# A mixture-of-experts decoder layer on one core: output projection by row tile, held expert loads, an early first down-projection, three blocks combined at the end

## The chip, the core and the metric

The kernel runs on one core of one Trainium2 chip. The core has a matrix engine (TensorE, PE in the rows; its weight loads are PEld), a vector engine (VectorE, DVE), an activation engine (ScalarE, ACT), GpSimd (POOL) and a queue engine (SyncE, SP) that issues most of the transfers. Each engine executes its own instructions in the order written and waits only on semaphores. The metric is device microseconds (us) of one execution of the whole layer.

## The reference

One layer on 512 tokens of width 1024, all in f32: `x` is normalised, a mixer with three branches gives `m`, and two residual steps follow.

```python
x = layer_norm(ALPHA * x + m, ln1_g, ln1_b)      # m = y @ w_o + b_o, the output projection
f = hierarchical_moe(x, ...)                     # router: best of 4 groups, best 2 of its 4 experts
x = layer_norm(ALPHA * x + f, ln2_g, ln2_b)
```

There are 16 experts. Each has an up-projection (1024 to 2 x 256, SwiGLU) and a down-projection (256 to 1024), 3 MB of weights. Every token is worked on by two experts, with a weight for each.

## The kernel before, in words

All large products are done in three passes (`mm3`, L107): each f32 operand is split into a high part, rounded for TensorE (a cast on ScalarE), and a low part, the difference (a subtraction on VectorE). The products high-high, high-low and low-high are summed. So each expert weight that arrives by DMA costs one cast and one subtraction of 128x1024 per quarter of the up-projection (`prep_hi` L752, `prep_lo` L761) and the same for each half of the down-projection (`dn_hi` L1194, `dn_lo` L1199).

From the line `late.enter_context(tc.manual_schedule())` on, the order of every engine's instructions is the order in which the program writes them. A helper `weave` spreads independent instructions between those of a dependent chain. The stages of this part are:

1. **Output projection.** Eight steps `i` of the loop over `2 * NT`. Each is 24 multiplications of one row tile `t` (128 tokens) with one column half `n`. `wo_add` (L792) adds the residual from PSUM, `wo_stats` takes statistics, `r_tr` (L805) transposes the result on TensorE in the next step, and `router` (L813) multiplies it with the router weights. Before, `n` is the outer index: the four row tiles of the first half, then the four of the second. A row tile is complete only when its second half is done, so its layer norm (`ln1_stats`, `center_ops`, `scale_ops`), its stores (`put_x1`) and its routing (`route_ops`) lie in steps 5 to 7 and behind the loop.
2. **Routing.** `rank_mm` counts tokens per expert, `pos_ops` makes one-hot rows, and `pick` (L885) multiplies the normalised tokens with them, which gives the first block's tokens already transposed, without a trip through memory. The other blocks' tokens are fetched by `gather` (L1081, an indirect DMA on GpSimd from `x1_d`).
3. **Expert blocks.** 18 blocks of up to 128 tokens (`seq`; experts 15 and 14 have two blocks each). A block is `up_mm` (24 multiplications, L109), the gated activation `gate_h` (L1173, L1174), a transposition `h_tr` (L1180) and its split `h_ev`, and `down_mm` (12 multiplications, L1217). In block `b` the weights of the next expert are split, the tokens of `b + 1` are transposed and split (`transp`, L1159), and the down-projection of `b - 1` is done. `down_ev` copies the result and `scatter` (L1230) adds it into `acc_d` with an indirect DMA. Scatters follow one another: each waits for the one before to land, since both add into the same rows.
4. **End.** The last two blocks are not scattered. Their results are split (`down_split`) and added to the tokens by a product with one-hot rows (`row_hot`, `combine`), after the sum so far has been read back (`acc_load`). The second layer norm and the stores follow.

Loads of expert weights (`load_unit`, L747) go through SyncE's queue in program order. Each needs a free buffer of a pool (`o` five, `raw` two, `rawx` two, `raw3` one). The split parts lie in `xp` (four buffers) and `hlp` (five), both named `hl`.

Of the kernel before, what the change touches and what calls it, by code (L numbers as in the profile page):

```python
# [53 lines left out]
def trunk(ctx, tc, x, mem, rows, cols, wz, wkv, pac, pb8, pb2, wax, ws, wo, wr, br, we, out):  # L54
# [120 lines left out]
    acc_d = dram.tile([T, D], F32, name="acc_d")  # L175

# [524 lines left out]
    def load_xr(i):  # L701
        n, t = divmod(i, NT)
# [75 lines left out]
    for e, u in ((1, 0), (1, 1), (1, 2), (2, 0), (2, 2)):  # L778
        load_unit(e, u)
# [3 lines left out]
    def wo_mm(i, ps, k0, k1):  # L783
        n, t = divmod(i, NT)
# [5 lines left out]
    def wo_add(i, ps):  # L790
        n, t = divmod(i, NT)
        dve.tensor_tensor(x1[:, t, n * 512:(n + 1) * 512], ps, xrs[i], op=ALU.add)  # L792

    def wo_stats(i):
        n, t = divmod(i, NT)
# [4 lines left out]
    def r_tr(i):  # L800
        n, t = divmod(i, NT)
# [7 lines left out]
    def router(i):  # L809
        n, t = divmod(i, NT)  # L810
# [10 lines left out]
    def logits_b(t):  # L821
        dve.tensor_tensor(ge[:, t, :], ge[:, t, :], routed[NT + t][:, :20], op=ALU.add)
# [83 lines left out]
    rest = []  # L906
    pending = {NT: [(2, 1)], NT + 1: [(3, 0), (3, 1)], NT + 2: [(4, 0)]}
    for i in range(2 * NT):
        j = i - 1
        t = j - NT  # L910
        ps = mmps()
        if i == 6:
            ohe = so2.tile([P, NT, P], F32, name="xr2")
        wo_mm(i, ps, 0, 2)
        if i:
            r_tr(j)
        if i in (NT + 1, NT + 2):
            for h in range(2):
                prep_hi(0, 2 * (i - NT - 1) + h)
        wo_mm(i, ps, 2, 4)  # L920
        if i:
            router(j)
        if t == 0:
            weave(ln1_stats(0))
        elif t == 1:
            weave(ln1_stats(1), scale_ops(0, 256, range(0, D, 256)))
            put_x1(sp, 0)
        elif t == 2:
            ops, r_ = route_ops(0, 2)
            rest += r_  # L930
            weave(ops, ln1_stats(2))
        if t >= 0:
            logits_a(t)
            weave(center_ops(t, D, (0,)))
            logits_b(t)
            if t:
                weave(scale_ops(t, 512, (0, 512)))
                put_x1(sp, t)
        wo_mm(i, ps, 4, 6)
        if t == 2:  # L940
            rank_mm(0)
            rank_mm(1)
            ops, r_ = route_ops(2, 3)
            rest += r_
            weave(ops, pos_ops(0, 2)[:2])
        wo_mm(i, ps, 6, 8)
        for e, u in pending.get(i, ()):
            load_unit(e, u)
# [625 lines left out]
```

## Time and profile before

| | |
|---|---|
| time, three runs | 924.68 us median, 920.58 to 927.96 |
| profiled execution | 922.9 us, of which the span of the trace is 921.2 us |
| busy: TensorE, weight load | 879.5 us (95%), 730.1 us (79%) |
| busy: VectorE, ScalarE, GpSimd | 583.9 us (63%), 460.5 us (50%), 58.7 us (6%) |
| mean granted TensorE clock | 0.982 |
| moved by DMA | 145.10 MB, mean 158 GB/s |

The span runs from the first to the last instruction; the execution's own time is 1.7 us longer. TensorE is busy almost everywhere: in the page's 40 slices of 23 us only three, from 691 to 760 us, and the last two fall below 9 tenths. A share of busy time is an average: where TensorE idles, the rows below name what it waited for. In a timeline row the columns are start, duration, engine, line, operation, tiles, shape and count, and in brackets the idle time before it with the releaser.

### The profile page before, as it was taken

How to read it: one execution, taken by the hardware profiler on the slowest of the kernel's cores; microseconds unless marked ns; L12 is line 12 of the kernel's file. 1: busy time of each engine (PE TensorE's matmuls, PEld its weight loads, DVE VectorE, ACT ScalarE, POOL GpSimd, SP SyncE). 2: the span in 40 equal slices, each digit the busy share in tenths (PEclk: the TensorE clock that was granted, in tenths of full speed). 3: DMA queues.
4: the chain of work that ended last, by engine and by line, in shares of the span. 5: the costliest groups of instructions: out<-in, count | busy, mean ns of one | idle time of the engine just before them, and what ended most of it. 6: DMA issues, size and time to landing. Idle time of an engine off the chain costs nothing. (4 is left out here: it accounts for less than half of the span.)

```text
span 921.2 us, 11143 instructions
## 1 busy us (share of the span) xinstructions
PE 879.5 (95%) x4256; PEld 730.1 (79%) x4256; DVE 583.9 (63%) x1010; ACT 460.5 (50%) x656; POOL 58.7 (6%) x60
## 2 busy tenths in 40 slices
PE   9999999999999999999999999999997889999981
PEld 5778888889998888888788888788877678888860
DVE  6756773344555543345866765765288987689966
ACT  5545432223444432215678687533023657688943
POOL 0000100000000000000000000000000122323210
PEclk9999999999999999999999999999998999999995
DMA  8313633323222313321313331338572787889565
GB/s 340 121 46 115 228 115 108 116 97 125 104 92 97 137 46 98 115 80 64 123 58 103 137 104 58 99 131 336 238 281 94 265 324 281 280 277 408 143 178 139
DMA packets 29424, 145.10 MB, mean 158 GB/s; under 512 B 5507, under 2 KB 5763, under 8 KB 16309
## 3 DMA queue, kind: packets, MB, share of 16 engines
q1 hardware_dynamic: 21460, 127.25, 38.0%
q0 software_dynamic: 6192, 13.84, 5.9%
q10 hardware_dynamic: 1712, 3.24, 1.1%
q8 instruction: 35, 0.57, 0.3%
q14 instruction: 25, 0.20, 0.1%
HBM read 136.24 MB, written 17.83 MB: 167 GB/s over the span
## 5 line engine op out<-in xcount | busy, mean ns | idle before, releaser
L109 PE MATMUL mm<-hl 128*128 128x512 f32 x1416 | 327.6, 390 | 0.2 <-DVE hl L83 0.2
L109 PEld LDWEIGHTS mm<-hl 128*128 128x128 f32 x1416 | 264.6, 188 | 54.7 <-DVE hl L83 0.6
L83 DVE TENSOR_TENSOR hl<-raw,hl 128x1024 fp32r<-128x1024 f32 (+1 forms) x116 | 136.2, 1180 | 136.4 <-ACT hl L82 135.9
L82 ACT CAST hl<-raw 128x1024 fp32r<-128x1024 f32 (+1 forms) x116 | 116.3, 1014 | 126.0 <-PE mm L109 113.8
L109 PE MATMUL mm<-o,hl 128*128 128x512 f32 x624 | 142.9, 389 | 1.2 <-ACT o L82 1.2
L109 PEld LDWEIGHTS mm<-o,hl 128*128 128x128 f32 x624 | 117.0, 188 | 25.9 <-ACT o L82 1.6
L109 PE MATMUL mm<-hl,xs 128*128 128x512 f32 x432 | 105.1, 399 | 1.1 <-DVE xs L83 1.1
L109 PEld LDWEIGHTS mm<-hl,xs 128*128 128x128 f32 x432 | 80.7, 191 | 18.1 <-DVE xs L83 1.8
L764 DVE TENSOR_TENSOR hl<-o,hl 128x1024 fp32r<-128x1024 f32 (+1 forms) x52 | 57.4, 1136 | 2.1 <-ACT hl L758 1.9
L1217 PE MATMUL mm<-hl,hT 128*128 128x512 f32 x196 | 49.8, 399 | 0.8 <-DVE hT L83 0.8
L758 ACT CAST hl<-o 128x1024 fp32r<-128x1024 f32 x48 | 47.9, 1052 | 1.7 <-PE mm L1217 1.7
L1217 PEld LDWEIGHTS mm<-hl,hT 128*128 128x128 f32 x196 | 35.5, 188 | 7.9 <-DVE hT L83 1.2
L1081 POOL DMA_INDIRECT y<-x_d,ixg x3 | 3.2, 1070 | 602.5 <-DVE rtl L1140 601.9
L223 ACT ACTIVATE gate<-mm,col 128x512 f32<-128x512 f32 x24 | 16.5, 688 | 39.6 <-PE mm L109 39.5
L1206 DVE TENSOR_TENSOR hl<-raw,hl 128x1024 fp32r<-128x1024 f32 x26 | 30.7, 1221 | 3.1 <-PE mm L109 1.6
L1197 ACT CAST hl<-raw 128x1024 fp32r<-128x1024 f32 x32 | 31.9, 1053 | 0.0
L109 PE MATMUL mm<-memT,hl 128*128 128x256 f32 x192 | 27.3, 286 | 0.2 <-ACT memT L82 0.2
L806 ACT COPY x1T<-aux 128x512 f32<-128x512 f32 x8 | 4.7, 587 | 45.5 <-PE aux L805 28.8
L307 PE MATMUL mm<-o,hl 128*128 128x512 f32 x96 | 25.4, 414 | 0.8 <-ACT hl L82 0.3
L109 PE MATMUL mm<-hl,yh 128*128 128x512 f32 x96 | 25.7, 414 | 0.0
L109 PEld LDWEIGHTS mm<-memT,hl 128*128 128x128 f32 x192 | 24.9, 191 | 0.9 <-ACT memT L82 0.4
L109 PE MATMUL mm<-hl,memT 128*128 128x256 f32 x192 | 24.3, 283 | 0.0
(333 smaller groups left out, 1125.9 us busy)
## 6 DMA issues: line engine op xcount, KB each, us to landing
raw<-in_wz_dram SPq DMA_DIRECT2D x30, 1024.0 KB, 4.8
o<-in_we_dram SPq DMA_DIRECT2D x24, 1024.0 KB, 7.8
raw<-in_we_dram SPq DMA_DIRECT2D x16, 1024.0 KB, 7.1
raw<-in_pac_dram SPq DMA_DIRECT2D x8, 1024.0 KB, 4.7
raw<-in_wkv_dram SPq DMA_DIRECT2D x8, 1024.0 KB, 4.7
rawx<-in_we_dram SPq DMA_DIRECT2D x8, 1024.0 KB, 4.9
raw<-in_pb_dram SPq DMA_DIRECT2D x4, 1024.0 KB, 6.0
raw<-in_wo_dram SPq DMA_DIRECT2D x4, 1024.0 KB, 4.9
```

Of the source, the lines that this page charges most:

```text
L82: act.copy(hi, src)
L83: dve.tensor_tensor(lo, src, hi.bitcast(F32), op=ALU.subtract)
L109: pe.matmul(ps, lhsT=a(sa_), rhs=b(sb_), start=first and i == 0, stop=last and i == 2)
L223: act.activation(store[j], ps, AF.Sigmoid, bias=cc(C_M + br_i * 8 + j))
L307: pe.matmul(ps, lhsT=xT(k, slice(t * P, (t + 1) * P))(sx), rhs=wv[2 * n + k // 4, k // 2 % 2][:, sw, k % 2, :], start=i == 0, stop=i == 23)
L758: act.copy(t[:, 0], raws[key, i // 2][:, (i % 2) * 1024:(i % 2 + 1) * 1024])
L764: (eng or dve).tensor_tensor(t[:, 1, c0:c1], src[:, c0:c1], t[:, 0, c0:c1].bitcast(F32), op=ALU.subtract)
L806: act.copy(x1T.rearrange("p k n -> p (k n)"), ps)
L1081: pool.indirect_dma_start(out=xg, out_offset=None, in_=x1_d[:, :], in_offset=bass.IndirectOffsetOnAxis(ap=ix[:, b:b + 1], axis=0), bounds_ ...
L1197: act.copy(dnh[key][:, :, n * 512:(n + 1) * 512], dn_half(key, n))
L1206: eng.tensor_tensor(dnl[key][n], dn_half(key, n), dnh[key][:, :, ns].bitcast(F32), op=ALU.subtract)
L1217: pe.matmul(ps, lhsT=hT[:, sa_, f, :], rhs=dn[sb_][:, f, :], start=i + f == 0, stop=i + f == 3)
```

## The change

The diff has four parts.

- **Output projection tile by tile.** Steps go `t` outer, `n` inner. Layer norm, store and routing of tile `t` stand in step `2 t + 2`; behind the loop only the last tile is left. Because both halves of `w_o` stay in use until the last two steps, expert 0's split weights go to the pool `o` instead of `xp`, and its raw units to `raw`.
- **Held loads.** Five units of experts 2 to 4, of which four were loaded during the output projection, are now issued in block 0, behind a tiny store `seen_d` that reads the gathered tokens of block 1. SyncE therefore waits there until that gather has landed. Units of expert 1 and others are loaded in steps 4 and 5.
- **First down-projection early.** Block 0 does its gate, transposition, down-projection and scatter itself, instead of in block 1.
- **Last three blocks combined.** Block 15 is split and combined like 16 and 17 instead of being scattered. A third one-hot table is made, one of them a block earlier. The pre-fill of `out` with the bias moves from block 16 to step 1 of the output projection.

The order on VectorE around the first complete row tile (`y` is the tile of projected tokens, `bnst`, `lnv`, `lnr`, `lnt` belong to the layer norm, `ge` are router logits). Before:

```order
L792 TENSOR_TENSOR y<-mm,xr 128x512
L798 BN_STATS bnst_4781<-y 128x6
L792 TENSOR_TENSOR y<-mm,xr 128x512
L798 BN_STATS bnst_4824<-y 128x6
L792 TENSOR_TENSOR y<-mm,xr_4721 128x512
L798 BN_STATS bnst_4867<-y 128x6
```

And now, the end of step 2 (its layer norm chain stands just ahead of these rows):

```order
L897 SCALAR_TENSOR_TENSOR y<-y,bnmv,g_4730 128x512 x2
L824 TENSOR_TENSOR ge<-ge,aux 128x20
L825 SCALAR_TENSOR_TENSOR ge<-ge,lnr_4854,cv 128x20
L901 SCALAR_TENSOR_TENSOR y<-y,lnr_4854,b_4732 128x512 x2
L767 TENSOR_TENSOR o<-raw,o 128x1024
L794 TENSOR_TENSOR y<-mm,xr_4722 128x512
```

The addition of step 2's result (the last row), for which TensorE's next transposition waits, now stands behind the layer norm of the tile before and one weight subtraction.

The order on TensorE in block 0 (`xs` are split tokens, `yb` here the low part of expert 0's down-projection, L1159/L1162 transposes the next tokens, L1180/L1183 transposes `h`). Before:

```order
L109 MATMUL mm<-hl,xs 128x512 x24
L1159 MATMUL aux<-ident,y 128x128 x8
L1050 MATMUL aux<-ohv_s,yb 128x12 x8
L109 MATMUL mm<-hl,xs 128x512 x24
L1180 MATMUL aux<-ident,h 128x128 x2
L1159 MATMUL aux<-ident,y 128x128 x8
L1217 MATMUL mm<-hl,hT 128x512 x4
L1217 MATMUL mm<-yb,hT 128x512 x2
```

And now, first TensorE and then ScalarE from the same place on:

```order
L109 MATMUL mm<-o,xs 128x512 x24
L1055 MATMUL aux<-ohv_s,yb 128x12 x8
L1183 MATMUL aux<-ident,h 128x128 x2
L1162 MATMUL aux<-ident,y 128x128 x8
L1220 MATMUL mm<-hl,hT 128x512 x4
L1220 MATMUL mm<-yb,hT 128x512 x2
L1220 MATMUL mm<-hl,hT 128x512 x4
L1220 MATMUL mm<-yb,hT 128x512 x2
L109 MATMUL mm<-hl,xs 128x512 x24
```

```order
L82 CAST hT<-aux 128x256
L82 CAST xs<-aux 128x512 x2
L1229 COPY yb<-mm 128x512 x2
L761 CAST hl<-rawx 128x1024 x2
L761 CAST hl<-o 128x1024 x2
```

The down-projection now stands between the up-projections of blocks 0 and 1, behind a transposition of `h` that has no other product ahead of it, and on ScalarE the copies of its result stand ahead of the casts of expert 2's weights.

The order on ScalarE in blocks 16 and 17 (`hl<-mm` is a split of a down-projection's result into the pool `xp`, `hl<-raw` the casts of down-projection weights). Before, and then now:

```order
L82 CAST xs<-aux 128x512 x2
L1387 DMA out_dram<-in_rows_dram 256x1024
L1226 COPY yb<-mm 128x512 x2
L82 CAST hT<-aux 128x256
L1197 CAST hl<-raw 128x2x512 x4
```

```order
L82 CAST xs<-aux 128x512 x2
L82 CAST hl<-mm 128x512 x2
L82 CAST hT<-aux 128x256
L1200 CAST hl<-raw 128x2x512 x2
L1200 CAST hl<-raw_6968 128x2x512 x2
```

The copy of block 15's result for the scatter has become a split into a buffer of `xp`, ahead of the last casts. That pool now holds the up-projection weights of the last expert, since key 0 no longer takes its turn in it.

The diff, without the repeated change of the index from `n, t = divmod(i, NT)` to `t, n = divmod(i, 2)` and without the renamed calls:

```diff
+    seen_d = dram.tile([1, 4], F32, name="seen_d")
     def load_unit(key, u):
-            if c % 7 > 4 and key < E:
+            if key == 0:
+                t = rawp.tile([P, 2048], F32, name="raw")
+            elif c % 7 in (3, 4) and key < E:
                 t = mox.tile([P, 2048], F32, name="rawx", bufs=2)
-            if c % 3 == 1 and key < E:
+            if c % 3 == 0 and key < E:
                 t = mlate.tile([P, 2048], F32, name="raw3")
     def prep_hi(key, i):
-            pools[key] = xp if counts["prep"] % 2 and key < E else hlp
-        t = pools[key].tile([P, 2, 1024], F32R, name="hl")
+            pools[key] = op_ if key == 0 else hlp if counts["prep"] % 2 or key >= E else xp
+        t = pools[key].tile([P, 2, 1024], F32R, name="hl" if key else "o")
-    for e, u in ((1, 0), (1, 1), (1, 2), (2, 0), (2, 2)):
-        load_unit(e, u)
+    load_unit(1, 0)
-    pending = {NT: [(2, 1)], NT + 1: [(3, 0), (3, 1)], NT + 2: [(4, 0)]}
+    pending = {4: [(1, 1), (2, 0)], 5: [(1, 2), (2, 2)]}
+    def ln1_tile(t, fill=()):
+        weave(ln1_stats(t), fill)
+        logits_a(t)
+        weave(center_ops(t, 512, (0, 512)))
+        logits_b(t)
     for i in range(2 * NT):
...
+        if 0 < i < 5:
+            prep_hi(0, i - 1)
...
+        if i and i % 2 == 0:
+            t = i // 2 - 1
+            ln1_tile(t)
+            weave(scale_ops(t, 512, (0, 512)))
+            put_x1(sp, t)
+        if 0 < i < 5:
+            prep_lo(0, i - 1)
+        if i == 5:
+            ops, rest = route_ops(0, 2)
+            weave(ops)
...
+        if i == 6:
+            weave(pos_ops(0, 2) + rest)
+        if i == 7:
+            ops, rest = route_ops(2, 3)
+            weave(ops)
...
+        if i == 1:
+            r = ROWS.index("ln2_b")
+            act.dma_start(out[:2 * P, :], rows[r:r + 1, :].to_broadcast([2 * P, D]))
         wo_add(i, ps)
         wo_stats(i)
     pick(0, 0, 8)
     r_tr(2 * NT - 1)
...
+    ln1_tile(t, pos_ops(2, 3))
     pick(1, 4, 8)
+    pick(2, 0, 8)
+    ops, rest3 = route_ops(t, NT)
+    weave(ops, scale_ops(t, 256, range(0, D, 256)))
     put_x1(sp, t)
     rank_mm(t)
     weave(pos_ops(t, NT))
     pick(t, 0, 8)
-    load_unit(4, 1)
         if b == 0:
+            sp.dma_start(seen_d, xgi[1][0:1, 0:4])
+            for e, u in ((2, 1), (3, 0), (3, 1), (4, 0), (4, 1)):
+                load_unit(e, u)
             dn_hi(0, 0)
             dn_hi(0, 1)
-            transp(1)
             pw = map_mm(ohs_s, NS, 1, 3)
             gws = map_gw(pw, NS, "s")
-        elif b == 1:
-            pth = h_tr(h)
+            h = gate_h(pu, gws, NS - 1)
+            hT = h_ev(h_tr(h))
+            dn_lo(0, 0, dve, None)
+            transp(1)
+            dn_lo(0, 1, dve, None)
+            pdn[0] = down_mm(0, hT)
+            scatter(down_ev(pdn[0]), *where(0)[::2])
-            r = ROWS.index("ln2_b")
-            act.dma_start(out[:2 * P, :], rows[r:r + 1, :].to_broadcast([2 * P, D]))
+        if b == nb - 4:
+            oht = mox.tile([P, 4, T], F32R, name="rawx", bufs=2)
+            row_hot(oht[:, 0], *where(nb - 3)[::2])
         if b == nb - 3:
-            for i in range(2):
-                row_hot(oht[:, i], *where(nb - 2 + i)[::2])
+            for i in range(1, 3):
+                row_hot(oht[:, i], *where(nb - 3 + i)[::2])
-        if b:
+        if b > 1:
             pdn[b - 1] = down_mm(b - 1, hT)
-            if b < 3 or b == nb - 2:
+            if b == nb - 2:
+                ys.append(down_split(pdn[b - 1]))
+            elif b < 3:
                 scatter(down_ev(pdn[b - 1]), *where(b - 1)[::2])
     def combine(t, n):
-        for i in range(2):
+        for i in range(3):
```

## Rows read from the trace of the kernel before

**Rows 1.** Table by stretch, columns: stretch, length, busy per engine, clock, DMA, GB/s.

```profile
681.50:709.60 28.10, 20.47 (x128) 18.79 (x129) 24.17 (x110) 5.50 (x9) 0.00 (x0) 0.82 0.47 184
709.60:744.50 34.90, 28.74 (x145) 22.72 (x144) 34.02 (x95) 23.66 (x35) 8.04 (x6) 1.00 0.73 263
744.50:868.30 123.80, 123.80 (x608) 103.01 (x608) 104.09 (x124) 94.62 (x140) 36.67 (x24) 0.99 0.85 292
```

**Rows 2.** Timeline of TensorE, end of the output projection to block 0.

```profile
683.55 1.11 PE L805 MATMUL aux<-ident,y 128*128 128x128 f32 x4 [2.06 <-DVE y L792]
684.31 2.82 PE L109 MATMUL mm<-hl,yh 128*128 128x512 f32 x6
...
693.29 3.43 PE L885 MATMUL mm<-xr,y 128*128 128x128 f32 x16 [2.33 <-DVE xr L880]
...
709.62 5.89 PE L109 MATMUL mm<-hl,xs 128*128 128x512 f32 x24
```

**Rows 3.** Timeline of VectorE, additions, first layer norm and last routing chain.

```profile
666.50 0.69 DVE L792 TENSOR_TENSOR y<-mm,xr 128x512 f32<-128x512 f32 x1 [5.39 <-PE mm L109]
...
671.29 0.24 DVE L823 SCALAR_TENSOR_TENSOR ge<-ge,lnr,cv 128x20 f32<-128x20 f32 x1
673.31 0.69 DVE L792 TENSOR_TENSOR y<-mm,xr 128x512 f32<-128x512 f32 x1 [1.78 <-PE mm L109]
...
681.48 1.41 DVE L899 SCALAR_TENSOR_TENSOR y<-y,lnr,b 128x512 f32<-128x512 f32 x2
...
700.02 0.17 DVE L847 TENSOR_TENSOR scr<-ge 128x16 f32<-128x16 f32 x1
...
704.24 0.18 DVE L861 TENSOR_TENSOR cnt<-r,goh 128x16 bf16<-128x16 f32 x1
```

**Rows 4.** Timeline of TensorE, blocks 1 and 2.

```profile
716.31 1.06 PE L1159 MATMUL aux<-ident,y 128*128 128x128 f32 x8 [0.81 <-DMA y<-x_d,ixg]
...
730.97 5.71 PE L109 MATMUL mm<-hl,xs 128*128 128x512 f32 x24
```

**Rows 5.** Timeline of VectorE, blocks 0 to 2.

```profile
716.78 2.35 DVE L764 TENSOR_TENSOR hl<-o,hl 128x1024 fp32r<-128x1024 f32 x2
...
723.38 0.17 DVE L1121 TENSOR_SCALAR nx<-ntot 128x16 f32<-128x16 f32 x1
...
734.82 0.42 DVE L83 TENSOR_TENSOR hT<-aux,hT 128x256 fp32r<-128x256 f32 x1
```

**Rows 6.** Timeline of ScalarE, casts of expert 2 and copies of block 0.

```profile
718.21 2.00 ACT L758 CAST hl<-o 128x1024 fp32r<-128x1024 f32 x2
...
728.65 0.59 ACT L1226 COPY yb<-mm 128x512 f32<-128x512 f32 x1 [1.68 <-PE mm L1217]
```

**Rows 7.** Transfers issued at 600 to 720 us: count, size, median to landing.

```profile
raw<-in_we_dram SPq DMA_DIRECT2D x3, 1024.0 KB, 10.4
```

**Rows 8.** Timeline of GpSimd, first gather and last scatters.

```profile
711.96 1.08 POOL L1081 DMA_INDIRECT y<-x_d,ixg  x1 [601.88 <-DVE rtl L1140]
...
878.19 1.55 POOL L1230 DMA_INDIRECT acc_d<-yb,ix_x  x1 [5.35 <-ACT yb L1226]
888.05 1.55 POOL L1230 DMA_INDIRECT acc_d<-yb,ix_x  x1 [8.30 <-ACT hl L82]
```

**Rows 9.** Timeline of all engines, last blocks and end.

```profile
870.53 0.88 DVE L1247 TENSOR_SCALAR rawx<-iof,nmr 128x128 fp32r<-128x128 f32 x4
...
877.86 0.44 PE L1180 MATMUL aux<-ident,h 128*128 128x128 f32 x2 [0.25 <-DVE h L1174]
...
889.33 2.99 PE L1430 MATMUL aux<-hl,rawx 128*128 128x512 f32 x12
...
894.17 1.75 SPq L1235 DMA_DIRECT2D y<-acc_d  x4
...
897.54 0.69 DVE L1432 SCALAR_TENSOR_TENSOR y<-aux,y 128x512 f32<-128x512 f32 x1 [6.70 <-DMA y<-acc_d]
...
899.62 0.69 DVE L1432 SCALAR_TENSOR_TENSOR y<-mm,y 128x512 f32<-128x512 f32 x1
```

More of the change, by code (lines that the diff above doesn't have):

```diff
@@ L783, in wo_mm @@
     def wo_mm(i, ps, k0, k1):
-        n, t = divmod(i, NT)
+        t, n = divmod(i, 2)
         for k in range(k0, k1):
@@ L790, in wo_add @@
     def wo_add(i, ps):
-        n, t = divmod(i, NT)
+        t, n = divmod(i, 2)
         dve.tensor_tensor(x1[:, t, n * 512:(n + 1) * 512], ps, xrs[i], op=ALU.add)
     def wo_stats(i):
-        n, t = divmod(i, NT)
+        t, n = divmod(i, 2)
         if n == 0:
@@ L800, in r_tr @@
     def r_tr(i):
-        n, t = divmod(i, NT)
+        t, n = divmod(i, 2)
         x1T = so.tile([P, 4, P], F32, name="x1T", bufs=1)
@@ L809, in router @@
     def router(i):
-        n, t = divmod(i, NT)
+        t, n = divmod(i, 2)
         ps = auxps()
@@ L904, in put_x1, with mm_pair @@
             eng.dma_start(d_[t * P:(t + 1) * P, :], x1[:, t, :])
-    rest = []
-    pending = {NT: [(2, 1)], NT + 1: [(3, 0), (3, 1)], NT + 2: [(4, 0)]}
+    pending = {4: [(1, 1), (2, 0)], 5: [(1, 2), (2, 2)]}
[4 more added lines that the diff above has]
+        logits_b(t)
+    def mm_pair(i, ps, q):
+        wo_mm(i, ps, 2 * q, 2 * q + 2)
     for i in range(2 * NT):
         j = i - 1
-        t = j - NT
@@ L911, in trunk @@
         ps = mmps()
+        mm_pair(i, ps, 0)
         if i == 6:
             ohe = so2.tile([P, NT, P], F32, name="xr2")
-        wo_mm(i, ps, 0, 2)
         if i:
             r_tr(j)
[L917 to L920, printed above, removed]
+        if 0 < i < 5:
+            prep_hi(0, i - 1)
+        mm_pair(i, ps, 1)
         if i:
             router(j)
[L923 to L931, printed above, removed]
@@ L941, in trunk @@
+        mm_pair(i, ps, 2)
+        if i == 5:
             rank_mm(0)
             rank_mm(1)
[L943 to L946, printed above, removed]
+        if i == 6:
[3 more added lines that the diff above has]
+            weave(ops)
+        mm_pair(i, ps, 3)
         for e, u in pending.get(i, ()):
             load_unit(e, u)
+        if i == 1:
+            r = ROWS.index("ln2_b")
+            act.dma_start(out[:2 * P, :], rows[r:r + 1, :].to_broadcast([2 * P, D]))
@@ L949, in trunk @@
+        if i == 7:
+            rank_mm(2)
         wo_add(i, ps)
         wo_stats(i)
-        if i in (NT + 1, NT + 2):
-            for h in range(2):
-                prep_lo(0, 2 * (i - NT - 1) + h)
         if i + 3 < 2 * NT:
@@ L959, in trunk @@
     r_tr(2 * NT - 1)
-    rank_mm(2)
-    weave(ln1_stats(t), pos_ops(0, 2)[2:] + pos_ops(2, 3) + rest)
     pick(1, 0, 4)
+    prep_hi(1, 0)
+    prep_hi(1, 1)
     router(2 * NT - 1)
+    ln1_tile(t, pos_ops(2, 3))
     pick(1, 4, 8)
-    logits_a(t)
-    logits_b(t)
-    ops, rest = route_ops(t, NT)
-    weave(ops, center_ops(t, 512, (0, 512)) + scale_ops(t, 512, (0, 512)))
+    pick(2, 0, 8)
+    ops, rest3 = route_ops(t, NT)
+    weave(ops, scale_ops(t, 256, range(0, D, 256)))
     put_x1(sp, t)
-    pick(2, 0, 4)
     rank_mm(t)
-    pick(2, 4, 8)
     weave(pos_ops(t, NT))
     pick(t, 0, 8)
+    weave(rest)
+    rest = rest3
     rtl = rt0.tile([P, 7, NT], F32, name="rtl")
@@ L1000, in trunk @@
     ]
-    prep_hi(1, 0)
-    prep_hi(1, 1)
     weave(first)
@@ L1369, in trunk @@
                     load_unit(order[i // 2], i % 2)
-        h = gate_h(pu, gw, c)
+        if b:
+            h = gate_h(pu, gw, c)
         if 0 < b < nb - 1:
@@ L1427, in combine @@
         ps = (mmps if n and t else auxps)()
-        for i in range(2):
+        for i in range(3):
             for k in range(2):
                 pe.matmul(ps, lhsT=oht[:, i, t * P:(t + 1) * P], rhs=ys[i][:, k, ns],
-                          start=i + k == 0, stop=i + k == 2)
+                          start=i + k == 0, stop=i + k == 3)
         dve.scalar_tensor_tensor(xs_[t][:, ns], ps, 1.0, xs_[t][:, ns], op0=ALU.mult, op1=ALU.add,
```

19 lines of the change are left out of this document (4 added, 15 removed).

## The prediction

> **What bounds the kernel now.** I read the table by stretch first, since one share for the whole span hides the stages [rows 1]. From 744.5 to 868.3 TensorE has no idle time at all at a clock of 0.99; an edit there gains nothing unless it removes products. From 681.5 to 709.6, between the last steps of the output projection and block 0, TensorE is busy 20.47 of 28.10 us, at a mean granted clock of 0.82, so partly at 1.2 instead of 2.4 GHz. From 709.6 to 744.5 it is busy 28.74 of 34.90 us, and VectorE 34.02: there VectorE sets the pace. The rest of the idle time lies behind 890 us. So three places can give time, and the timelines say what each waits for.
>
> The TensorE timeline [rows 2] shows a wait of 2.06 us for an addition (`y L792`) in the last step, after which six products take 2.82 us, about twice what 24 in 5.71 us gives [rows 4], and a wait of 2.33 us for the first one-hot rows. The products of the output projection thus end at 693.29 - 2.33 = 690.96, and block 0 starts at 709.62, 18.7 us later. In that gap VectorE does the last tile's layer norm and its routing, one short dependent instruction after the other [rows 3]. At the end [rows 8, 9] the chain is a transfer: block 15's scatter is issued at 888.05, the sums are read back at 894.17, and VectorE, 6.70 us idle, starts at 897.54, although TensorE began to combine at 889.33.
>
> **The change, part by part.** All times are on the scale of the trace before.
>
> *Output projection.* A step takes 6.81 us, the distance of two additions [rows 3]. Undisturbed, the products would end 0.2 us before the addition at 673.31 plus two steps: 686.7. Now VectorE has a layer norm in steps 2, 4 and 6. From an addition to the finished logits takes 671.29 + 0.24 - 666.50 = 5.03 us (0.1 more with the centering in halves), scaling 1.41 [rows 3], one weight subtraction 2.35 / 2 = 1.18 [rows 5]. That is 7.7 us, so the step's own addition comes 0.9 us late. TensorE asks for it only after six more products (6 x 0.238 = 1.43 us, from 5.71 / 24 [rows 4]), and the addition takes 0.69: a wait of about 0.4 us, hidden down to that by the six products. Step 6 has one-hot rows in place of the subtraction; I take 0.6. Three waits make 1.4 us, and the products end at **688.1** instead of 690.96. Bounds: 686.7 with none; a wait of 2.06 in each is the third rival.
>
> *Last tile and routing.* Addition to logits again, 5.2 us, with 0.3 for two woven instructions: 693.9 with the lag of 0.2 and rounding. The routing chain took 704.24 + 0.18 - 700.02 = 4.40 us, woven with four operations of 0.7 us [rows 3]. Now centering is ahead of it (inside the 5.2), and the four fills are half as wide, so I take 4.40 - 4 x 0.25 = 3.4, and 4.4 as its other bound: 697.3. From there to block 0 it was 709.62 - 704.42 = 5.2 us [rows 2, 3]; five small instructions come in, 0.1. Block 0 starts at **702.6**: 7.0 us earlier, of which 2.8 are from the projection.
>
> *Blocks 0 to 2.* Most of VectorE's list is moved, not shortened, and it is what bounds. From block 0's start to the end of expert 1's subtractions it took 716.78 + 2.35 - 709.62 = 9.5 us [rows 2, 5]: now 712.1. Then follow, on an almost bare chain, the gate weights and gate (0.8), `h`'s transposition and split over three engines (1.3), half of the down weights (1.2), the next tokens' low parts (1.2), the other half (1.2): 717.8. The early down-projection ends there, and TensorE, which idles some 3 us behind block 0's products, gets to block 1 at 718.3, with block 0's down-projection already done. Next late is ScalarE: its copies of that result, 0.59 each, stand ahead of expert 2's casts of 1.0 each [rows 6], so the first cast ends at 719.9 and VectorE, ready at 717.8, idles 2.1 us. From there the old list took 734.82 - 723.38 = 11.4 us to the next split of `h` [rows 5], less 0.3 for the one that has left it: 731.0, and it was 734.82. By TensorE's path (VectorE's gate, 5.9 us after that first cast, then `h`'s transposition) block 2 starts at 726.7, where it was 730.97 [rows 4]. These give 3.8 and 4.3; I take **4.0 us**. So 3 of the 7 us are given back. If the two idle times did not come, all 7 would stay; if the clock fell with TensorE's idle 3 us and its products became the bound, 1 to 2 more would go, about the extra 2.82 - 1.43 of the six slow products [rows 2].
>
> *Held loads.* The first gather was issued at 711.96 and its tokens used at 716.31 [rows 4, 8], 4.35 us; issued at about 704.7 it lands at 709.1, and then SyncE issues the five units. Behind that wait stand only weight loads. The first, expert 2's second half, is needed by its cast at about 721. The slowest class of such loads landed 10.4 us after issue in the median [rows 7], so at 719.5: covered by 1.5 us, and the others are needed 8 us and more later. Price 0. Without the hold the loads could not start much earlier anyway, since their buffers hold expert 0's weights until block 0's products, 702.6 to 708.5, have used them. The Trainium skill says the opposite of this edit (DMA: Bandwidth & Descriptors, section Rules for kernel authors): issue a DMA early, compute, and wait on it late. By that rule the sum would lose what the load is late; the cover above says none, and no run here shows it yet.
>
> *From block 3 on* TensorE is full; the shift of 4.0 is carried along. VectorE is busy 104.09 of 123.80 us there in all, but almost wholly in full blocks.
>
> *The end.* A third one-hot table costs 0.88 us and a conversion on VectorE [rows 9], a block earlier. Block 16 already waited 0.25 us for its gate then; I take 0.8 more. Block 15's split, with its 1.28 us of VectorE, needs a buffer that the last expert's weights hold until TensorE is 1.4 us into block 17, and ScalarE's last casts stand behind it: 1.1 more. So TensorE begins to combine at 889.33 + 1.9 = 891.2. Each of eight parts has now six products, 1.4 us, instead of four. The first needs the last split, as before: done at 892.9, and the fourth at 897.0, so VectorE has its fourth part by 897.8. Before, it was 899.62 + 0.69 = 900.3. The sums are there by then: block 14's scatter was issued at 878.19 and followed 9.9 us later by the next, which waits for it [rows 8]; reading back took 897.54 - 894.17 = 3.4, so 891.5. **2.5 us** gained. The bounds are 0 and the 6.0 that the missing scatter gives alone (897.54 - 891.5). The pre-fill of `out`, moved to step 1, hides behind a stage whose transfers are not waited for.
>
> **Sum.** 4.0 + 2.5 = 6.5 us from the profiled execution's 922.9 gives 916.4. The median of the runs is 1.8 above that execution: 924.7 - 6.5 = **918.2**.
>
> **The rivals.**
> 1. *The early start is kept.* VectorE finds its casts ready, block 2 starts 7 us earlier, and the end gives 6: 13 us, 911.7. For it: the split of `h` and the tokens of block 1 are only 0.8 us of TensorE wait now [rows 4]. Against it: ScalarE's order, which is fixed.
> 2. *The scatters eat it.* Each waits for the one before, 9.9 us at the end [rows 8], more than a block. If they do not shift with TensorE, the sums come at 891.5 on the old scale whatever the blocks do, and the gain is what the missing scatter gives, at most 6.0, and with slower blocks 3: 921 to 922.
> 3. *Slower: VectorE in the output projection.* If the layer norm makes the addition late by 1.6 us more than I find, each of three waits is the 2.06 us of [rows 2], and the clock falls after it as it did there, 1.4 us on the next six products and as much on the following: 3 x (2.06 + 2.8) = 14.6 instead of 1.4. Block 0 would start at 715.8, 6.2 later than before, block 2 some 9 later, less 2.5 at the end: 931. It decides where VectorE's work in such a step passes about 9.3 us instead of my 7.7.
> 4. *Slower: held loads come late.* Each us that expert 2's second half lands after 721 delays block 2. Over 6.5 us late, after 727.5, the change is slower; at 732, 5 us slower, 929. That needs over 18 us to land; nothing in [rows 7] is near. The rule of the Trainium skill named above (DMA: Bandwidth & Descriptors, Rules for kernel authors) would expect this case.
> 5. *The change does not do what it says:* the hold changes no order of landing because the buffers bind. Then nothing in the sum changes.
>
> **How the numbers follow.** Forecast, 3 to 9 us gained: 0.57. Rival 1, 9 to 15: 0.22. Rival 2 and other losses that leave 0 to 3: 0.12. Rivals 3 and 4 with others of their sign: 0.06 and 0.03. Rival 5 lies inside the first. One per cent, 9.2 us, is about what a measurement of this kernel can tell from no change: three runs lay between 920.58 and 927.96. Faster by over 1% is rival 1, with its lower edge given to both cases: 0.24; slower by over 1%, which the prices of rivals 3 and 4 reach only with a further stall: 0.05; within: 0.71. The range leaves out the slower rivals and the last of rival 1: 910 to 925.
>
> **What would show it.** Right: block 0's products start 6 to 8 us earlier, block 2's only 3 to 5; TensorE idle about 3 us ahead of L1183 in block 0; VectorE idle about 2 us ahead of expert 2's first subtraction, released by ScalarE; the additions in steps 2, 4 and 6 directly behind a subtraction, with waits of TensorE under 1 us and the clock at 1.00; no wait for the held loads; at the end L1444 not waiting for a transfer, but for L1442. Wrong: a step of the projection with a wait over 2 us, casts of expert 2 waiting for a DMA, or idle time of TensorE between 745 and 860.

## The result and the profile after

The changed kernel takes **918.76 us** in the median of five runs (917.83 to 920.99); the kernel before, run five times beside it, takes 924.68 (920.58 to 927.96). The ratio is 0.994, with a 95% interval of 0.9922 to 0.9958. It is 5.9 us faster; 6.5 were forecast, and 918.2 us.

The profiled execution of the changed kernel is the longest of its five, 920.99 us with a span of 919.2; the one of before was 1.8 us under its median. So the two traces differ by only 1.9 us where the medians differ by 5.9, and what follows compares stretches, not spans. Step 0 of the output projection starts at 633.96 in the trace after and at 633.56 in the one before: 0.4 us has to be taken off where absolute times are compared (below: on the old scale).

The table by stretch [rows 1], with the same columns, cut at the same events:

```profile
681.50:702.80 21.30, 19.07 (x132) 17.20 (x131) 16.58 (x81) 6.50 (x11) 0.00 (x0) 0.90 0.26 106
702.80:741.20 38.40, 31.55 (x143) 25.20 (x144) 33.57 (x94) 23.27 (x34) 8.15 (x6) 0.90 0.90 344
741.20:865.80 124.60, 124.60 (x607) 103.65 (x608) 104.03 (x128) 94.51 (x140) 35.04 (x25) 0.98 0.85 290
```

The way to block 0 has become 6.8 us shorter, the way from block 0 to block 3 3.5 us longer (34.9 to 38.4), and from there TensorE is full, as before. The timeline of TensorE says where [rows 2, 4]:

```profile
697.22 0.17 PE L877 MATMUL aux<-cnt,low 128*128 128x16 bf16 x1 [1.65 <-DVE cnt L863]
...
702.79 8.59 PE L109 MATMUL mm<-o,xs 128*128 128x512 f32 x24
...
713.22 0.44 PE L1183 MATMUL aux<-ident,h 128*128 128x128 f32 x2 [1.05 <-DVE h L1177]
...
718.61 5.64 PE L109 MATMUL mm<-hl,xs 128*128 128x512 f32 x24
...
727.50 5.74 PE L109 MATMUL mm<-hl,xs 128*128 128x512 f32 x24
...
738.97 0.44 PE L1183 MATMUL aux<-ident,h 128*128 128x128 f32 x2 [2.12 <-DVE h L1177]
...
741.24 8.15 PE L109 MATMUL mm<-hl,xs 128*128 128x512 f32 x24
...
753.88 5.72 PE L109 MATMUL mm<-hl,xs 128*128 128x512 f32 x24
```

The last three rows of products are those of blocks 2, 3 and 4. In the trace before, blocks 3 and 4 were:

```profile
744.49 7.35 PE L109 MATMUL mm<-hl,xs 128*128 128x512 f32 x24
...
756.34 5.72 PE L109 MATMUL mm<-hl,xs 128*128 128x512 f32 x24
```

Block 0 starts 6.8 us earlier, block 2 3.5 (730.97 before), block 4 only 2.5. Blocks 0 and 3 need 8.59 and 8.15 us for 24 products that take 5.7 elsewhere. The table by stretch for TensorE alone, 1 us each (after the busy time: clock, DMA, GB/s), has the two ends of the first slow part:

```profile
698.00:699.00 1.00, 1.00 (x7) 0.82 1.04 426
699.00:700.00 1.00, 1.00 (x7) 0.50 1.03 422
...
708.00:709.00 1.00, 1.00 (x4) 0.56 0.92 283
709.00:710.00 1.00, 1.00 (x6) 1.00 1.22 197
```

The granted clock is 0.50 (1.2 GHz) for some 10 us there, behind an idle time of 1.65 us, and again from 739.6 to 746.4, behind one of 2.12 us. In the trace before it was so four times between 683 and 749 us, for some 3.4 us each, the last time in block 3.

ScalarE and VectorE between blocks 0 and 2 [rows 5, 6], first ScalarE:

```profile
716.48 0.59 ACT L1229 COPY yb<-mm 128x512 f32<-128x512 f32 x1 [1.27 <-PE mm L1220]
718.81 0.59 ACT L1229 COPY yb<-mm 128x512 f32<-128x512 f32 x1 [1.74 <-PE mm L1220]
719.29 2.00 ACT L761 CAST hl<-rawx 128x1024 fp32r<-128x1024 f32 x2
```

```profile
716.77 1.22 DVE L1209 TENSOR_TENSOR yb<-raw,hl 128x1024 fp32r<-128x1024 f32 x1
717.91 0.17 DVE L1126 TENSOR_SCALAR nx<-ntot 128x16 f32<-128x16 f32 x1
720.38 0.69 DVE L767 TENSOR_TENSOR hl<-rawx,hl 128x512 fp32r<-128x512 f32 x1 [2.30 <-ACT hl L761]
```

That is the forecast wait: VectorE has nothing to do for 2.30 us, as the casts of expert 2 stand behind two copies that wait for TensorE. All engines at the end [rows 8, 9]:

```profile
872.20 4.55 POOL L1233 DMA_INDIRECT acc_d<-yb,ix_x  x1 [5.35 <-ACT hl L761]
...
885.14 1.22 DVE L1209 TENSOR_TENSOR o<-raw,hl 128x1024 fp32r<-128x1024 f32 x1
...
886.42 0.81 SPq L1392 DMA_DIRECT2D raw<-in_rows_dram  x2
...
887.40 2.17 SPq L1238 DMA_DIRECT2D y<-acc_d  x4
...
888.33 4.24 PE L1442 MATMUL aux<-hl,rawx 128*128 128x512 f32 x18
...
893.60 0.69 DVE L1444 SCALAR_TENSOR_TENSOR y<-aux,y 128x512 f32<-128x512 f32 x1 [3.76 <-DMA y<-acc_d]
...
895.68 0.69 DVE L1444 SCALAR_TENSOR_TENSOR y<-mm,y 128x512 f32<-128x512 f32 x1
```

TensorE combines from 888.33 on, and VectorE still waits 3.76 us for the read-back, although block 14's scatter was issued 15 us before. The read-backs stand on SyncE behind the loads of the last layer norm's gains and biases, which wait for their buffer until the subtraction at 885.14. In the trace before, these loads were issued 12 us earlier, and the read-backs behind them (894.17) waited for block 15's scatter:

```profile
874.04 1.61 SPq L1382 DMA_DIRECT2D raw<-in_rows_dram  x2
```

VectorE's last instruction ends at 910.73, 3.9 us earlier than before (914.65).

### The profile page after: what moved, and what is told of

The parts are those of the page before. It is cut to its first block, busy times and chain, and to the rows that moved or that the text cites. A ratio compares the mean times of both kernels' runs of the same rounds, so it can differ in the third digit from the quotient of the medians.

```text
span 919.2 us, 11177 instructions
## 1 busy us (share of the span) xinstructions
PE 883.4 (96%) x4272; PEld 733.8 (80%) x4272; DVE 588.8 (64%) x1020; ACT 460.6 (50%) x656; POOL 58.1 (6%) x59
## 4 chain that ended last, share of the span: by engine, by line
PE 78%; DVE 11%; ACT 5%; DMA 3%; issue 2%; SPq 0%; DVEq 0%; ACTq 0%
PE mm L109 61%; PE mm L1220 4%; PE aux L109 4%; PE mm L308 3%; DVE hl L767 2%; PE aux L1162 1%; DMA x<-in_x_dram 1%; DMA col<-in_cols_dram 1%; ACT hl L82 1%; PE aux L1442 1%; DMA o<-in_we_dram 1%; DVE hl L83 1%; PE aux L464 1%; DVE xs L83 1%; ACT hl L1200 1%
## 5 line engine op out<-in xcount | busy, mean ns | idle before, releaser
L109 PE MATMUL mm<-hl,xs 128*128 128x512 f32 x408 | 99.7, 401 | 0.0
L109 PEld LDWEIGHTS mm<-hl,xs 128*128 128x128 f32 x408 | 77.1, 193 | 15.9
L767 DVE TENSOR_TENSOR hl<-o,hl 128x1024 fp32r<-128x1024 f32 (+1 forms) x45 | 50.3, 1147 | 4.8 <-ACT hl L761 4.7
L761 ACT CAST hl<-o 128x1024 fp32r<-128x1024 f32 x42 | 41.9, 1051 | 4.2 <-PE mm L1220 4.2
```

The costliest lines, as they stand in the source:

```text
L109: pe.matmul(ps, lhsT=a(sa_), rhs=b(sb_), start=first and i == 0, stop=last and i == 2)
L761: act.copy(t[:, 0], raws[key, i // 2][:, (i % 2) * 1024:(i % 2 + 1) * 1024])
L767: (eng or dve).tensor_tensor(t[:, 1, c0:c1], src[:, c0:c1], t[:, 0, c0:c1].bitcast(F32), op=ALU.subtract)
```

## The experiments

Times are medians; the difference is to the kernel before, measured beside each kernel: 924.68 for the changed kernel, 924.63 for the next four, 923.61 for the four after that and 925.43 for the last four. Kernels of different groups are compared by these differences. "Late down" is block 0's down-projection where it was before.

| kernel | us | to before | ratio, 95% interval |
|---|---|---|---|
| changed kernel | 918.76 | -5.9 | 0.9940 (0.9922 to 0.9958) |
| gains behind read-backs | 920.91 | -3.7 | 0.9954 (0.9936 to 0.9973) |
| casts first | 916.57 | -8.1 | 0.9913 (0.9888 to 0.9938) |
| late down | 915.43 | -9.2 | 0.9907 (0.9881 to 0.9932) |
| two-block combination | 920.20 | -4.4 | 0.9960 (0.9942 to 0.9977) |
| no hold | 919.35 | -4.3 | 0.9953 (0.9937 to 0.9969) |
| filled idle times | 917.83 | -5.8 | 0.9934 (0.9910 to 0.9957) |
| gains in another buffer | 917.61 | -6.0 | 0.9927 (0.9905 to 0.9948) |
| late down, buffer, one fill | **910.63** | -13.0 | 0.9854 (0.9826 to 0.9881) |
| late down, buffer | 913.96 | -11.5 | 0.9883 (0.9854 to 0.9911) |
| late down, buffer, two fills | 911.43 | -14.0 | 0.9860 (0.9833 to 0.9888) |
| late down, buffer, one fill, no hold | 916.75 | -8.7 | 0.9904 (0.9870 to 0.9937) |
| late down, no hold, two-block combination | 922.03 | -3.4 | 0.9968 (0.9948 to 0.9987) |

**Casts first.** ScalarE's copies and the scatter move behind the casts:

```diff
             pdn[0] = down_mm(0, hT)
-            scatter(down_ev(pdn[0]), *where(0)[::2])
...
                 prep_hi(nxt, 3)
+            if b == 1:
+                scatter(down_ev(pdn[0]), *where(0)[::2])
```

> The changed kernel with ScalarE's two copies of block 0's down-projection (and its scatter) behind the four casts of expert 2's weights, not ahead of them. My theory: these copies, which wait for TensorE, are what VectorE waits 2.30 us for at 720.4. Then that wait is under 0.3, block 2 starts at about 725.5 instead of 727.5, and the time falls by 2 us, to 916.8. Rival A, the clock: TensorE's granted clock falls to 1.2 GHz again ahead of block 3, whose products then take 8 us, and block 4 is shifted by less than 1 us: 918 to 919. Rival B, the casts of the second half then wait for the held load instead: VectorE idle about 1 us, 917.8.

Measured 916.57 (915.74 to 917.34; the changed kernel's lowest was 917.83). VectorE's wait at that place is gone, and block 2 starts 3.0 us earlier; 2.1 of them arise between the starts of blocks 1 and 2 (6.8 us instead of 8.9), the rest was there before. TensorE's timeline:

```profile
717.70 5.60 PE L109 MATMUL mm<-hl,xs 128*128 128x512 f32 x24
...
724.49 5.94 PE L109 MATMUL mm<-hl,xs 128*128 128x512 f32 x24
...
736.21 0.44 PE L1183 MATMUL aux<-ident,h 128*128 128x128 f32 x2 [2.17 <-DVE h L1177]
...
738.48 8.23 PE L109 MATMUL mm<-hl,xs 128*128 128x512 f32 x24
```

Block 3 is again at the low clock, but it was so in the changed kernel too, and block 4 (751.21) keeps 2.7 of the 3.0 us. The wait for the copies was real and on the path: 2.2 us by the differences, as expected, with intervals of the ratios that overlap.

**Late down.** Block 0's gate, transposition and down-projection go back to block 1; only `transp(1)` stays, ahead of the gate weights. The lines taken out:

```diff
-            h = gate_h(pu, gws, NS - 1)
-            hT = h_ev(h_tr(h))
-            dn_lo(0, 0, dve, None)
-            transp(1)
-            dn_lo(0, 1, dve, None)
-            pdn[0] = down_mm(0, hT)
-            scatter(down_ev(pdn[0]), *where(0)[::2])
```

> The changed kernel with block 0's gate, transposition and down-projection back where they were: behind block 1's products, VectorE's two subtractions of expert 0's down weights in block 1. My theory: of the 7 us that block 0 starts earlier, the early down-projection gives back 3, so that without it block 2 starts at about 724.5 instead of 727.5 and the time falls by 3 us, to 915.8. Rival A: it gives nothing back, since the same work only moves, and the time stays within 0.7 us of 918.8. Rival B: it is worth something, because block 1's list on VectorE is then longer and is what block 2 waits for: 920 to 922.

Measured 915.43 (914.46 to 917.61): 3.3 us less. TensorE's timeline:

```profile
701.63 5.75 PE L109 MATMUL mm<-o,xs 128*128 128x512 f32 x24
708.48 1.06 PE L1162 MATMUL aux<-ident,y 128*128 128x128 f32 x8 [1.10 <-DMA y<-x_d,ixg]
...
711.67 5.29 PE L109 MATMUL mm<-hl,xs 128*128 128x512 f32 x22 [0.76 <-DVE xs L83]
...
723.02 5.71 PE L109 MATMUL mm<-hl,xs 128*128 128x512 f32 x24
```

Block 2 starts at 723.02 instead of 727.50. Of these 4.5 us, 1.2 are there at block 0's start already, since in this execution the clock stayed at 1.00 there; from block 0's start to block 2's it is 21.4 us instead of 24.7. TensorE goes from block 0's products almost straight to block 1's, and the chain over gate, transposition, split and subtractions runs beside them. What it waits for now is the first gather, 1.10 us.

**No hold.** Only the tiny store is taken out.

```diff
-            sp.dma_start(seen_d, xgi[1][0:1, 0:4])
```

> The changed kernel without the small transfer that SyncE holds the five expert loads for. My theory: the hold costs nothing and gives nothing, since the buffers of these loads are not free earlier and no cast waits for them: 918.8, within 0.9. Rival A, the rule of issuing a transfer early: the loads start some us earlier, expert 2's second half is there earlier, 917 or less. Rival B: the loads, no longer held, take the channel from the gathers of the second block's tokens; TensorE waits for these tokens behind block 0, 1 to 3 us: 920 to 922.

Measured 919.35, not told from the changed kernel (4.3 under the kernel before, against 5.9). But my reason was half wrong. The five loads are issued at 705.34 instead of 708.93, so they could start earlier. And the three gathers land 4.5, 10.3 and 12.6 us after issue (least, median, most), with the hold 4.3, 6.2 and 6.9. Nobody sees it here, because in this order TensorE asks for the tokens late. In the order with the late down-projection it asks for them at once, so I took the hold away there (same edit):

> The kernel of three edits (910.6) without the hold of the five expert loads. In the run without the hold the loads were issued 3.6 us earlier, and the three gathers landed 10.3 us after issue in the median where it was 6.2; nobody waited for them there, since block 1 came late. In the kernel of three edits TensorE waits 0.81 us for the first gather. My theory: the hold protects the gathers, and without it TensorE waits 3 to 5 us there, of which VectorE's list hides some: 912 to 914. Rival A: VectorE's list hides all of it, 910.6. Rival B: the loads that start 3.6 us earlier give something back to expert 2's casts, 909 to 910.

Measured 916.75, 5.3 us more than the kernel with two fills on the same chip (911.43), six runs each; one of the six took 910.98. (By the differences it is 4.3 us more than the kernel with one fill, from which it differs by the hold alone.) TensorE's timeline of this kernel, and then of the same kernel with the hold (one fill):

```profile
702.48 5.71 PE L109 MATMUL mm<-o,xs 128*128 128x512 f32 x24
713.78 1.94 PE L1162 MATMUL aux<-ident,y 128*128 128x128 f32 x8 [5.58 <-DMA y<-x_d,ixg]
```

```profile
702.64 5.90 PE L109 MATMUL mm<-o,xs 128*128 128x512 f32 x24
709.36 1.06 PE L1162 MATMUL aux<-ident,y 128*128 128x128 f32 x8 [0.81 <-DMA y<-x_d,ixg]
```

The gathers land 9.0, 11.5 and 14.4 us after issue, and the wait grows from 0.81 to 5.58. The mechanism was as expected, its size larger than the 912 to 914 I gave it: VectorE's list hid none of it.

**What the projection order is worth without the rest.** Late down, no hold and two-block combination together:

> The changed kernel with three of its parts undone together: block 0's down-projection back behind block 1's products, no hold of the expert loads, only the last two blocks combined. What is left is the order of the output projection with the shorter routing (and the buffers that go with it). My theory: these are worth 7 us at block 0 and keep them when the early down-projection is gone (which alone gave 3.3 us back), less 1.4 for the two-block end and 0 to 3 for tokens that land later without the hold: 917 to 920. Rival A: without the hold nothing is lost and the scatters bind the end, 916 to 917. Rival B: the early start is lost altogether, 922 or more.

Measured 922.03, more than the 917 to 920 expected, with 10 of 12 runs at 920.45 to 923.99 and two at 914.73 and 916.47. The profiled one is the lowest; in it TensorE does not wait for the gather at all. That is a step of some 6 us, as in the kernel without the hold just above: by the two traces, an execution in which the first gather lands in time and one in which it doesn't. No trace of an execution at 922 was taken, so for this kernel that is inferred, and what the projection order alone is worth stays open.

**Filled idle times.** Products that nothing reads, six ahead of the last counting, eight each ahead of the transpositions in blocks 1 and 2 (the loop that adds them):

```diff
+        for _ in range(n):
+            pe.matmul(ps, lhsT=w[:, 0, :P], rhs=w[:, 0, :512], start=True, stop=True)
```

> The changed kernel with products added whose results nothing reads, in TensorE's three idle times of 1.65 to 2.2 us (six ahead of the last tile's counting, eight each ahead of the transpositions of block 1's and block 2's gates), some 0.24 us each, so that they fit in. My theory: TensorE's granted clock falls to 1.2 GHz after such an idle time, and block 3's 24 products at 8.15 us instead of 5.7 cost the most; with the fill they take 5.7 to 6, block 4 starts 2 to 2.5 us earlier and the time is 916.5. Rival A: VectorE, not the slow products, sets the pace to block 4 (its list there is nearly without idle time): block 3's products are fast but block 4 starts within 0.7 us of before, 918.5. Rival B: the fill itself makes TensorE late where it stands, 919 to 921.

Measured 917.83, not told from the changed kernel. With the first fill the clock stayed at 1.00 up to block 0's end, as it also did in three of the eleven traces without it; block 0 took 5.75 us and started at 701.35. It did not help, since VectorE's list was the pace: TensorE then idled 3.76 us ahead of L1188 (the transposition of block 0's `h`), and the clock was 0.50 from 709.7 to 716.5. Block 1 started at 717.86. In block 3 the clock fell too, at 740.4, behind idle times of only 0.31 and 0.60 us, and its products took 7.34.

**Gains and biases.** Moved behind the read-backs, and then into another buffer:

```diff
-            load_gb(sp, 0)
-            load_gb(sp, 1)
...
     for t in range(NT):
         acc_load(t)
+    load_gb(sp, 0)
+    load_gb(sp, 1)
```

> The changed kernel with one thing moved: the two loads of the last layer norm's gains and biases are issued behind the four read-backs of the sums, not ahead of them. In the changed kernel the read-backs stand on SyncE behind these loads, which wait until 886.4 for a buffer; they land at 893.5, and VectorE waits 3.76 us for them. My theory: that order, not the scatter, is what is late. Then the read-backs are issued by about 882 and land by 888, VectorE's first sum waits for TensorE alone (about 891), its fourth is done about 894.6 instead of 896.4, and the time falls by 1.7 us, to 917.1. Rival A, the scatter of block 14 itself lands late: the first sum still waits for the read-back at 893, 918.8. Rival B, the gains now arrive late, and the centering waits for them: 918.8 to 920.

Measured 920.91. The wait changed its name (VectorE):

```profile
891.61 0.69 DVE L1444 SCALAR_TENSOR_TENSOR y<-aux,y 128x512 f32<-128x512 f32 x1 [2.06 <-DMA y<-acc_d]
...
898.62 1.41 DVE L1453 SCALAR_TENSOR_TENSOR o<-y,ln2s,raw 128x512 f32<-128x512 f32 x2 [3.98 <-DMA raw<-in_rows_dram]
```

In this execution block 14's scatter was issued only at 881.74, where the trace of the changed kernel has it at 872.20; the read-backs followed at 888.34, so VectorE still waited for the scatter (rival A), and the gains came behind them (rival B).

```diff
-            gb2 = mlate.tile([P, 2048], F32, name="raw3")
+            gb2 = rawp.tile([P, 2048], F32, name="raw")
```

> The changed kernel with the last layer norm's gains and biases in another buffer, one that is free some 12 us earlier (that of an expert before the last), so that their loads no longer hold SyncE until 886.4; the read-backs behind them then wait for the scatter of block 14 alone. My theory after the run that moved them: the scatters' chain, which varies from execution to execution, and this order each bind in some executions; without the order, the best times fall by 1 to 1.7 us and the median by about 1, to 917.8. Rival A: the order alone is what binds in most executions, 917.1. Rival B: the scatters alone bind, and the time is 918.8 to 920.

Measured 917.61, not told from the changed kernel (6.0 under the kernel before, against 5.9). Here too the scatter was late, at 882.11, so the gains, issued at 872.03, were no longer what held the read-backs (888.61).

**Two-block combination.** Block 15 is scattered again; the parts of the change on the one-hot tables, `down_split` and the range in `combine` are undone.

> The changed kernel with only the last two blocks combined on the chip again, block 15 scattered as before. My theory: the third block in the combination is worth 2.5 us or somewhat more, so 921.3 to 922; VectorE's first sum then waits for the read-back behind block 15's scatter, at about 895 to 896, though TensorE begins to combine 1 to 2 us earlier. Rival A: the chain of scatters was not what bound the end, and the third block only costs (0.8 for its table, 1.1 for its split): 917. Rival B: without it the sums come a whole scatter later (10 us), and the time is 925 or more.

Measured 920.20: 1.5 us more than the changed kernel by the differences, with intervals that overlap. TensorE combines at 885.47 (block 4 started 1.4 us earlier in this trace, so 1.5 us of the 2.9 are the third block's own cost), but VectorE waits 5.46 us for the read-back, until 892.44. That is no later than with the third block (893.60), so by these traces and medians it is not shown that the third block gains anything; the 2.5 us or more expected are not there.

**Together.** Late down, the other buffer, and eight products ahead of block 2's transposition; then without the fill; then with a second fill ahead of the last counting:

> Three edits together on the changed kernel: block 0's gate and down-projection where they were before (measured alone at 915.4), the gains and biases in the earlier buffer, and eight products that nothing reads ahead of the transposition of block 2's gate, where TensorE is idle 2.07 us. My theory: 915.4 less 2 for the clock ahead of block 3 and less 0.8 for the read-backs, 912.6. Rival A: VectorE sets the pace to block 4 and the scatters the end, 915 to 916. Rival B: an earlier TensorE meets scatters that have not shifted, and the whole gain of the fill turns into a longer wait for the read-back: 914.5 to 915.5.

> The changed kernel with block 0's down-projection where it was before and the gains and biases in the earlier buffer, without any product added: it tells what the eight added products ahead of block 2's transposition are worth in the kernel of three edits, at 910.6. My theory: block 3's products take 8 us again at the clock of 1.2 GHz, block 4 starts 2 us later, and the time is 913.5 to 914.4 (915.4 less 1 to 1.2 for the buffer). Rival A: the added products do nothing, and the gain was the buffer's: 910.6. Rival B: the buffer gains nothing in this order, 915.4.

> The kernel of three edits (910.6) with six more products that nothing reads, in TensorE's idle time of 1.65 us ahead of the last tile's counting. There the following 16 small products took 3.59 us at the lower clock and block 0 started at 702.64; in a run where the clock had stayed up they took 2.05 and it started at 701.63. My theory: 1 us, 909.6. Rival A: block 1 waits for its gathered tokens and VectorE for its own list, so that the 1 us is lost there: 910.6. Rival B: the fill itself delays the counting by more than it saves, 911 to 912.

Measured 910.63 (912.6 expected), 913.96 (as expected) and 911.43 (909.6 expected). On one chip the two fills together are worth 2.5 us (911.43 against 913.96). The other buffer gives 2.3 us by the differences (-11.5 against -9.2), with overlapping intervals. TensorE's timeline without a fill and with the one:

```profile
736.81 0.44 PE L1183 MATMUL aux<-ident,h 128*128 128x128 f32 x2 [2.03 <-DVE h L1177]
...
738.92 7.31 PE L109 MATMUL mm<-hl,xs 128*128 128x512 f32 x24
...
750.74 5.72 PE L109 MATMUL mm<-hl,xs 128*128 128x512 f32 x24
```

```profile
733.17 1.98 PE L1183 MATMUL aux<-hl 128*128 128x512 f32 x8
735.43 0.44 PE L1185 MATMUL aux<-ident,h 128*128 128x128 f32 x2 [0.28 <-DVE h L1177]
...
737.54 5.71 PE L109 MATMUL mm<-hl,xs 128*128 128x512 f32 x24
...
747.75 5.72 PE L109 MATMUL mm<-hl,xs 128*128 128x512 f32 x24
```

With the fill, the clock in the second trace is 1.00 from 702 us on, and from the transposition to block 4 it is 12.3 us instead of 13.9. In the kernel without a fill the scatter was early (868.26), and for once the end is TensorE's (VectorE):

```profile
888.17 0.69 DVE L1440 SCALAR_TENSOR_TENSOR y<-aux,y 128x512 f32<-128x512 f32 x1 [0.66 <-PE aux L1438]
```

The second fill gave nothing that can be told (ratios 0.9854 and 0.9860): rival A. With one fill or two the kernel is 13 to 14 us under the kernel before, and 7 to 8 under the changed one.

## Why the prediction was right, and where not

The additions on VectorE at every second step, by which the first point goes (trace after):

```profile
646.41 0.69 DVE L794 TENSOR_TENSOR y<-mm,xr 128x512 f32<-128x512 f32 x1 [2.22 <-PE mm L109]
...
660.45 0.69 DVE L794 TENSOR_TENSOR y<-mm,xr 128x512 f32<-128x512 f32 x1 [2.22 <-PE mm L109]
...
674.67 0.69 DVE L794 TENSOR_TENSOR y<-mm,xr 128x512 f32<-128x512 f32 x1 [2.94 <-PE mm L109]
...
688.57 0.69 DVE L794 TENSOR_TENSOR y<-mm,xr 128x512 f32<-128x512 f32 x1 [2.94 <-PE aux L875]
```

- **Output projection: right.** The products end at 688.5, 688.1 on the old scale as forecast. Two steps take 14.04, 14.22 and 13.90 us from addition to addition instead of 13.62, so the three waits sum to 1.3 (forecast 1.4), at a clock of 1.00.
- **Block 0's start: right.** 702.79, 702.4 on the old scale (forecast 702.6).
- **Block 0 to 2: right in sum, with one piece not seen.** Its products ran at 1.2 GHz and took 8.59 us; the forecast had 5.9 and 3 us of idle time behind, and only 1.05 us of it came. The two fill the same gap: where the products took 5.75 to 5.9 (four other runs), TensorE idled 3.73 to 3.77 us ahead of the transposition, and block 1 came at 717.7 to 719.6, as in the changed kernel (718.6). VectorE's chain sets the pace, as written. Block 1 at 718.2 (forecast 718.3), VectorE's idle 2.30 (2.1), block 2 3.9 us earlier (4.0), all on the old scale. The late-down run puts 3.3 us on "3 of the 7 us are given back", the casts-first run 2 us on ScalarE's order.
- **"From block 3 on the shift of 4.0 is carried along": missed by 1 us.** Block 3 ran at 1.2 GHz for longer than before (8.15 against 7.35 us), and 2.5 us (2.9 on the old scale) came through. Measured from the end of the projection's products, block 4 starts 65.35 us later, and before it was 756.34 - 690.96 = 65.38. So by these traces everything that the shorter routing gained is given back between blocks 0 and 4, and what stays, 2.9 us, is the projection's own part. With the late down-projection it is 60.5, with one fill and the other buffer too 59.0.
- **Held loads: price right, reason wrong.** No cast waited for them, and 919.35 without the hold is no difference that can be told. But the hold does change when the loads start, and it shields the gathers. The rule of the Trainium skill (DMA: Bandwidth & Descriptors, Rules for kernel authors), to issue a DMA early and wait late, did not pay here: issued 3.6 us earlier, the loads took nothing off VectorE's wait for expert 2's casts (2.41 us instead of 2.30), and in the order that waits for the tokens this cost 5.3 us.
- **The end: mis-sized.** "The sums are there by then" failed. I had them at 887.5 (891.5 less 4.0); the read-backs landed at about 893.5. I had not seen that the new rule for `raw3` hands the gains' buffer to the last expert and so puts SyncE's read-backs behind it, and I took one time for block 14's scatter, which is issued anywhere between 867 and 882 in these traces. VectorE's fourth part is done 3.9 us earlier than before (4.3 on the old scale) instead of 6.5. The 1.9 us for table and split were right in kind (TensorE combines at 888.33; less the shift that had come through, 1.5 us later). Which of the two late things costs the median is not shown: with the order of the loads taken away the time cannot be told from the changed kernel's (917.61), and in the one execution of that kernel with a trace the scatter was late. The two-block run puts 1.5 us on the third block, not 2.5, and that is not told from nothing.
- **The total: in part luck.** The two terms were 4.0 and 2.5 us; the traces show 2.9 and 1.5 on the old scale, 4.3 in all before rounding. Both were taken too high, and that the medians differ by 5.9 is due to something that neither term holds.
- **What the traces leave open.** Up to VectorE's last instruction they show 3.9 of the medians' 5.9 us on their own scales. From the end of the last store's issue to the end of the span it is 7.9 us in the trace after and 6.2 in the one before, 6.3 to 7.7 in the twelve others; the change does not edit these stores. How early scatters run in an execution, which the profiled one can't stand for, is the likely rest, and isn't shown.

Rival 1 (all 7 us kept) fell with the early down-projection (3.3 us, of which ScalarE's order is some 2) and block 3's clock; rival 2 is true in part, as the read-back is what VectorE waits for in all but one of the fourteen traces.

## What to carry to other kernels

An earlier start is worth only what the next bound engine can take over: ask, engine by engine, what becomes late next, down to the clock of the engine that gets idle time. Two edits can guard the same wait: here the hold and the early down-projection both cover the gathered tokens. Taking away the hold alone changed nothing that can be told, taking away the early down-projection alone gained 3.3 us, and without either the wait was there: only one of them is needed, the cheap one. When a buffer rule changes, follow the new holder to its last use and look at what stands behind the waiting transfer on its queue.

## What the runs showed of the hardware

- **The clock after idle time is not the same from trace to trace.** Behind the same idle time of 1.66 us ahead of the last counting, the 16 small products took 2.05 us in three traces and 2.56 to 3.64 in eight. Behind idle times of 2.2 us ahead of block 2, its products took 5.7 us in two traces of the early down-projection and 7.16 to 7.33 in three. In the order with the late down-projection, block 3's products took 5.71 to 5.75 us with eight added products ahead of the transposition before them (three traces) and 7.31 to 7.98 without (three traces); in the order with the early one they took 7.34 with them.
- **Gathers are slowed by loads issued beside them.** Their median from issue to landing went from 6.2 to 10.3 and from 6.5 to 11.5 us, with five loads of 1 MB issued in the same few us.
- **An accumulating scatter late in the kernel** occupies GpSimd for 1.5 to 7.2 us. In three kernels that are alike up to some 870 us (changed kernel and the two with moved gains), block 14's was issued at 872.20, 881.74 and 882.11. The difference begins two scatters earlier: block 12's was issued at 858.47, 858.63 and 859.23 and occupied GpSimd for 1.60, 7.19 and 6.92 us. Why is not shown.
